# Plain slabs and weight sums of channel mixers 1 to 3 made one mixer ahead and kept in DRAM, in a two-layer decoder trunk on Trainium2

## The chip, the cores and the metric

The kernel runs on one core of a Trainium2 chip (trn2). The metric is the device time in microseconds of one execution, as the median of several runs. The core's engines work side by side, each on its own list of instructions in order: PE (TensorE) multiplies, DVE (VectorE) and ACT (ScalarE) work on tiles, POOL (GpSimd) does small things and starts some transfers, SP (SyncE) starts nearly all loads. A tile lies in SBUF, or in PSUM where PE writes it; DRAM is reached by DMA only.

## The reference

x has 512 tokens of 1024 numbers in fp32. Two layers follow, each with a channel mixer, a token mixer (latent attention in the first layer, sparse attention in the second) and another channel mixer, and a last norm ends it:

```
h = h + 1/2 * SwiGLU_a(RMSNorm(h))
h = h + Mixer_i(RMSNorm(h))
h = h + 1/2 * SwiGLU_b(RMSNorm(h))

def swiglu(x, w_gate, w_up, w_down):
    return (jax.nn.silu(x @ w_gate) * (x @ w_up)) @ w_down
```

The hidden width of SwiGLU is 2816. So there are four channel mixers, numbered 0 to 3 here; 0 opens layer 0, 1 closes it, 2 opens layer 1, 3 closes it.

## The kernel before

**Numbers.** Every fp32 operand of a matmul is split in two: ACT copies it to a rounded `hi` (L176, for a slab of weights L149), DVE subtracts that from the source for `lo` (L177, L151). Each product is then three matmuls: hi·hi, hi·lo, lo·hi (L168 to L170, L367 to L369, L379 to L381).

**A channel mixer** (`ffn`, L383) goes through the hidden width in 22 blocks of 128. The first blocks (`PLAIN`: 3 in mixer 0, 2 in the others) are *plain*: the gate slab (z = 0) and the up slab (z = 1) of a block, 128x1024 each, are loaded by SP (512 KB, tile wr, two buffers), split into one of three rotating weight tiles w0 to w2, and multiplied, 48 matmuls of 128x256 columns each.

The blocks behind them take seven products instead of eight (a Strassen-Winograd scheme of 2x2 blocks). `wsums` loads a block's gate slab rg and up slab ru, DVE makes four sums of halves (L353: s1; L354: into ru; L356, L357: into rg), and slabs and sums are split into the operands w[1] to w[7]. In the first product block ru, like every rg, lies in the ring `fr` with three buffers, in the others in wr; s1 has one buffer. `combine` makes the matching combinations of the input (tiles y, u and `four`; L242 to L244). The products run in the order 1, 7, 6, 2, 5, 4, 3, with 12 matmuls of 128x256 each; between them ACT copies px to pg (L497), pq to uq (L499) and px to uq (L501). Product 6 writes px again, so it waits for L497. uq has one buffer.

Product 1 needs only rg's split. Product 7 needs ru's, after a sum; product 6 that of the sums in rg.

**The norm.** The gate needs each token's 1/rms as a row. POOL takes a power (L282), DVE transposes the result (L290), two small POOL transfers spread it over the partitions (L291, L293). Then the plain blocks are finished (`plain_acts`, issued in the first product block): DVE multiplies the gate by the row (L395), ACT takes silu (L396), DVE multiplies by the row again (L397) and by the up half (L406, tile tu), ACT and DVE split that (ah, al).

**The down projection** runs in units of three blocks (wdr loads L425, matmuls, add L419), eight units spread over each three blocks.

**What sets the order.** The instructions of each engine are put in order by the scheduler of the tile framework, before the run; the program's text, priorities and `issue_after` lines steer it. On the chip each engine, and each queue of loads, keeps that order: an instruction that waits holds all that stand behind it. A load that waits for a buffer to come free also holds all behind it on SP.

Of the kernel before, what the change touches and what calls it, by code (L numbers as in the profile page):

```python
# [11 lines left out]
F32 = mybir.dt.float32  # L12
# [3 lines left out]
ALU = mybir.AluOpType  # L16
AX = mybir.AxisListType

P = 128
S = 512  # L20
D = 1024
KC = D // P
# [25 lines left out]
HS = S // 2  # L48
KP = KC // 2
PLAIN = 3, 2, 2, 2  # L50
PAD = 16
URGENT = 400
SHIFT = 1, 5, 7
TILES = 24
XC = P + 2
NG = 3
# [4 lines left out]
def f32v(ap):  # L61
    return ap.bitcast(F32)


class Kern:
# [13 lines left out]
    def setup(self):  # L79
        nc, cp, a = self.nc, self.cp, self.a  # L80

        self.nw, self.odd, self.nq = 0, 0, 0
        self.first = self.wp.tile([P, 2048 + 3 * PAD], F32R, tag="w0", name="w")
        small = self.wp.tile([P, 80], F32, name="small")
        self.vtc, self.small_sums, self.stc = small[:, :12], small[:, 12:16], small[:, 32:]
        self.sts, self.nst = [small[:, 12 + 4 * i : 16 + 4 * i] for i in range(5)], 0
        self.gains = cp.tile([P, 64], F32, name="gains")
        nc.scalar.dma_start(self.gains[:, :53], a["gains"])  # L90
        self.ident = cp.tile([P, P], F32, name="ident")
        nc.scalar.dma_start(self.ident, a["c_ident"])
        self.ones = cp.tile([P, P], F32R, name="ones")
        nc.vector.memset(f32v(self.ones), 1.0)
        nc.scalar.dma_start(self.gains[:, 53:57], a["c_rvalid"])
        tiny = self.gains[:, 57:62]
        nc.scalar.activation(tiny[:, 0:1], f32v(self.ones)[:, 0:1], AF.Copy)
        self.tiny = tiny
        self.root = self.gains[:, 62:63]
        nc.gpsimd.memset(self.root, -0.5)  # L100

        self.ngains = cp.tile([P, 32], F32, name="ngains")
        for i, x in enumerate(FGAINS):
            nc.vector.tensor_scalar(self.ngains[:, 8 * i : 8 * i + 8], self.gains[:, GAINS[x] : GAINS[x] + 8], -1.0, None, op0=ALU.mult)
        self.h, self.ahead, self.softmax, self.turn, self.chain, self.chained = [], [], False, 0, None, False
        self.h = [self.hp.tile([P, S], F32, name=f"h{c}") for c in range(KC)]
# [93 lines left out]
    def norm_split(self, c):  # L200
        t = self.xp.tile([P, 2 * S], F32R, tag="x", bufs=KC, name="x")
        if self.to_ffn:

            g = self.ngains[:, self.nng + c : self.nng + c + 1]
            v = t.rearrange("p (e z n) -> p e z n", e=2, z=2)
            hi, lo, src = v[:, :, 0, :], v[:, :, 1, :], self.h[c].rearrange("p (e n) -> p e n", e=2)
            self.split(src, hi, lo, gain=g)
            for e in range(2):
                self.xc["LR"[e], c] = v[:, e, 0, :], v[:, e, 1, :]
        else:  # L210
            self.split(self.h[c], t[:, :S], t[:, S:], gain=self.gains[:, self.ng + c : self.ng + c + 1])
            self.xh.append(t[:, :S])
            self.xl.append(t[:, S:])
# [104 lines left out]
    def sum_tiles(self, n):  # L318
        self.nsum += 1
        hi = self.fp.tile([P, n], F32R, tag="fh", bufs=3, name="wh")  # L320
        return hi, self.fp.tile([P, n + 2 * PAD], F32R, tag="fl", bufs=3, name="wl")[:, 2 * PAD :]

    def wsums(self, idx, f):


        nc, fp, w_gu = self.nc, self.fp, self.a["w_gu"]
        rg = fp.tile([P, 1024], F32, tag="fr", bufs=3, name="rg")
        nc.sync.dma_start(rg, w_gu[idx, f, 0])
        if f == PLAIN[idx]:

            ru = fp.tile([P, 1024], F32, tag="fr", bufs=3, name="ru")
        else:
            ru = self.wp.tile([P, 1024], F32, tag="wr", bufs=2, name="wr")
        nc.sync.dma_start(ru, w_gu[idx, f, 1])
        s1 = fp.tile([P, S], F32, tag="s1", bufs=1, name="s1")
        g0, g1, u0, u1 = rg[:, :S], rg[:, S:], ru[:, :S], ru[:, S:]

        def split(src, pool, tag, bufs):
            n = src.shape[1]
            if pool is self.wp:  # L340
                hi, lo = self.wtiles("half")
            elif n == 1024:
                hi, lo = self.sum_tiles(n)
            else:
                hi = pool.tile([P, n], F32R, tag=tag[0], bufs=bufs, name="wh")
                lo = pool.tile([P, n + 2 * PAD], F32R, tag=tag[1], bufs=bufs, name="wl")[:, 2 * PAD :]
            self.split(src, hi, lo)
            return [(hi[:, x : x + S].rearrange("p (k c) -> p k c", c=P), lo[:, x : x + S].rearrange("p (k c) -> p k c", c=P))
                    for x in range(0, n, S)]

        w = {}
        w[1], w[2] = split(rg, self.wp, None, 2)
        nc.vector.tensor_tensor(s1, u0, u1, op=ALU.add)  # L353
        nc.vector.tensor_tensor(u0, u0, g0, op=ALU.add)  # L354
        w[7], w[4] = split(ru, fp, ("fh", "fl"), 3)
        nc.vector.tensor_tensor(g0, g0, s1, op=ALU.add)  # L356
        nc.vector.tensor_tensor(g1, g1, g0, op=ALU.add)  # L357
        w[6], w[3] = split(rg, fp, ("fh", "fl"), 3)
        w[5], = split(s1, fp, ("sh", "sl"), 2)
        return w  # L360

    def product(self, j, w, out, first, last):
        mm = self.nc.tensor.matmul
        wh, wl = w[j]
        for p in range(KP):
# [2 lines left out]
            mm(out, wh[:, p], xl, start=False, stop=False, skip_group_check=True)  # L368
            mm(out, wl[:, p], xh, start=False, stop=last and p == KP - 1, skip_group_check=True)  # L369

    def plain(self, idx, f, z, out):

        wh, wl = self.ahead.pop(0) if self.ahead else self.wslab(self.a["w_gu"][idx, f, z], (KC, P), "half")
        mm = self.nc.tensor.matmul
        for k in self.order:
            for e in range(2):
                (xh, xl), o = self.xc["LR"[e], k], out[:, e * HS : e * HS + HS]

                mm(o, wh[:, k], xh, start=(k == 0 and e == 0), stop=False, skip_group_check=True)  # L379
                mm(o, wh[:, k], xl, start=False, stop=False, skip_group_check=True)  # L380
                mm(o, wl[:, k], xh, start=False, stop=(k == KC - 1), skip_group_check=True)  # L381

    def ffn(self, idx, gain_next, ap, tp):  # L383
        nc, a = self.nc, self.a
# [97 lines left out]
        for f in range(plain, NF):  # L482
# [3 lines left out]
            n = -(-len(units) // left)  # L486
# [23 lines left out]
            for work, tag in zip(todo, "oTS"):  # L510
                work(tag, copied if tag == "S" else None)
            act(f)
        if gain_next == "fin":

            hs, out = [self.parts(self.four(F32)) for _ in range(4)], []
            for t in range(4):
                for b in range(2):
                    p = self.mm_bank("ph")
                    for c in range(4):
                        nc.tensor.transpose(p[:, c * P : (c + 1) * P], self.h[4 * b + c][:, t * P : (t + 1) * P], self.ident)  # L520
                    out.append(hs[t][b])
                    nc.scalar.activation(out[-1], p, AF.Copy)
            return self.last(a["w_last"], ah, al, ap, out, hs)
# [921 lines left out]
```

## Time and profile before

| | us |
|---|---|
| median of 3 runs | 1857.13 (1856.23 to 1857.48) |
| the profiled execution | 1856.59 |
| its span, first to last instruction | 1854.8 |
| PE busy in it | 1834.9 |
| DVE busy | 1529.3 |
| ACT busy | 1091.9 |

A row of a group of instructions in the profile gives the line, the engine, the operation, out<-in, the shape, the count and the busy time. In a timeline the columns are the start and the length in us, and in brackets stands how long the engine was idle before it and for what. Tiles are named as in the program. Mean granted clock of the core: 0.999 of full speed.

### The profile page before, as it was taken

The numbers are of one execution on the slowest core, as the hardware profiler recorded it, in microseconds if no ns is written. First come the engines' busy times: TensorE is split into PE (matmuls) and PEld (weight loads), VectorE is DVE, ScalarE is ACT, GpSimd is POOL, SyncE is SP. The second block draws the span as 40 slices with busy tenths as digits, with TensorE's granted clock in tenths as the row PEclk, the third lists the DMA queues.
The fourth block names the chain that finished last, engine by engine and source line by source line (L and its number), as shares of the span: only waits on it lengthen the run. The fifth ranks groups of instructions, "written<-read, shape, count | busy, mean of one in ns | idle before, by whom it ended". The sixth has DMA issues, their size and how long they took to land.

```text
span 1854.8 us, 32725 instructions
## 1 busy us (share of the span) xinstructions
PE 1834.9 (99%) x12392; PEld 1675.0 (90%) x12392; DVE 1529.3 (82%) x2773; ACT 1091.9 (59%) x2030; POOL 251.5 (14%) x350
## 2 busy tenths in 40 slices
PE   8999999999999999999999999999999999999998
PEld 8999999888889999998999999988888889999997
DVE  7988886588789988887998888755988989988885
ACT  8555554489776555555655555426977865555554
POOL 0000000156510000000000000015665500000000
PEclk9999999999999999999999999999999999999999
DMA  7333333142333333333233333233222124333321
GB/s 259 118 103 102 103 107 108 56 107 71 96 115 113 104 110 111 111 106 100 97 116 107 107 104 97 90 106 108 75 86 75 46 106 137 103 107 103 103 91 57
DMA packets 79213, 191.12 MB, mean 103 GB/s; under 512 B 10024, under 2 KB 38080, under 8 KB 79056
## 3 DMA queue, kind: packets, MB, share of 16 engines
q1 hardware_dynamic: 75280, 182.42, 31.1%
q10 hardware_dynamic: 3104, 5.03, 0.8%
q8 instruction: 97, 1.59, 0.3%
q0 software_dynamic: 672, 1.59, 0.3%
q14 instruction: 60, 0.49, 0.1%
HBM read 179.75 MB, written 2.18 MB: 98 GB/s over the span
## 4 chain that ended last, share of the span: by engine, by line
PE 86%; DVE 8%; ACT 3%; issue 1%; DMA 1%; POOL 0%; SPq 0%; ACTq 0%; POOLq 0%; DVEq 0%
PE pd L168 8%; PE pd L170 8%; PE pd L169 8%; PE px L367 5%; PE px L369 5%; PE px L368 5%; PE pg L367 4%; PE pg L369 4%; PE pg L368 4%; PE pq L369 4%; PE pq L368 4%; PE pq L367 4%; PE o L1248 2%; PE pt L1223 2%; PE po L168 2%; PE po L170 2%
## 5 line engine op out<-in xcount | busy, mean ns | idle before, releaser
L169 PE MATMUL pd<-al,wd 128*128 128x512 f32 x576 | 224.1, 389 | 0.0
L168 PE MATMUL pd<-ah,wd 128*128 128x512 f32 x576 | 224.0, 389 | 0.0
L170 PE MATMUL pd<-ah,wd 128*128 128x512 f32 x576 | 224.0, 389 | 0.0
L177 DVE TENSOR_TENSOR w<-rg,w 128x1024 fp32r<-128x1024 f32 x79 | 96.6, 1223 | 104.4 <-ACT w L176 104.4
L367 PE MATMUL px<-four,wh 128*128 128x256 f32 x632 | 175.5, 278 | 4.0 <-ACT pg L497 3.8
L367 PE MATMUL pq<-four,wh 128*128 128x256 f32 x632 | 174.5, 276 | 0.3 <-DVE tu L406 0.3
L369 PE MATMUL px<-four,wl 128*128 128x256 f32 x632 | 174.7, 276 | 0.1
L368 PE MATMUL px<-four,wh 128*128 128x256 f32 x632 | 174.6, 276 | 0.0
L368 PE MATMUL pq<-four,wh 128*128 128x256 f32 x632 | 174.4, 276 | 0.0
L369 PE MATMUL pq<-four,wl 128*128 128x256 f32 x632 | 174.4, 276 | 0.0
L419 DVE SCALAR_TENSOR_TENSOR h<-pd,h 128x512 f32<-128x512 f32 x216 | 147.4, 683 | 6.0 <-PE pd L170 6.0
L176 ACT ACTIVATE wd<-wdr 128x384 fp32r<-128x384 f32 x192 | 98.5, 515 | 66.9 <-PE pd L169 35.9
L170 PEld LDWEIGHTS pd<-ah,wd 128*128 128x128 f32 x576 | 108.1, 188 | 22.5
L168 PEld LDWEIGHTS pd<-ah,wd 128*128 128x128 f32 x576 | 108.1, 188 | 19.5
L169 PEld LDWEIGHTS pd<-al,wd 128*128 128x128 f32 x576 | 108.1, 188 | 19.5
L367 PEld LDWEIGHTS px<-four,wh 128*128 128x128 f32 x632 | 118.6, 188 | 5.6 <-ACT pg L497 4.9
L367 PEld LDWEIGHTS pq<-four,wh 128*128 128x128 f32 x632 | 118.6, 188 | 0.5 <-ACT w L176 0.5
L369 PEld LDWEIGHTS px<-four,wl 128*128 128x128 f32 x632 | 118.6, 188 | 0.3 <-DVE wl L177 0.3
L369 PEld LDWEIGHTS pq<-four,wl 128*128 128x128 f32 x632 | 118.6, 188 | 0.0
L368 PEld LDWEIGHTS px<-four,wh 128*128 128x128 f32 x632 | 118.6, 188 | 0.0
L368 PEld LDWEIGHTS pq<-four,wh 128*128 128x128 f32 x632 | 118.6, 188 | 0.0
L176 ACT ACTIVATE w<-rg 128x1024 fp32r<-128x1024 f32 x79 | 83.7, 1060 | 57.5 <-PE pg L369 54.5
(363 smaller groups left out, 5942.1 us busy)
## 6 DMA issues: line engine op xcount, KB each, us to landing
wr<-in_w_gu SPq DMA_DIRECT2D x93, 512.0 KB, 4.1
rg<-in_w_gu SPq DMA_DIRECT2D x79, 512.0 KB, 3.3
wdr<-in_w_down SPq DMA_DIRECT2D x192, 192.0 KB, 2.4
wdr<-in_w_down SPq DMA_DIRECT2D x24, 256.0 KB, 2.7
wr<-in_mla_w_o SPq DMA_DIRECT2D x8, 512.0 KB, 3.5
wr<-in_nsa_w_q SPq DMA_DIRECT2D x8, 512.0 KB, 3.6
th<-btab_d SPq DMA_DIRECT2D x16, 256.0 KB, 3.6
wr<-in_nsa_w_o SPq DMA_DIRECT2D x8, 512.0 KB, 3.5
```

Of the source, the lines that this page charges most:

```text
L168: mm(out, wh, xh, start=first, stop=False)
L169: mm(out, wh, xl, start=False, stop=False)
L170: return mm(out, wl, xh, start=False, stop=last)
L176: nc.scalar.activation(hi, src, AF.Copy)
L177: (nc.gpsimd if pool else nc.vector).tensor_tensor(lo, src, f32v(hi), op=ALU.subtract)
L367: mm(out, wh[:, p], xh, start=first and p == 0, stop=False, skip_group_check=True)
L368: mm(out, wh[:, p], xl, start=False, stop=False, skip_group_check=True)
L369: mm(out, wl[:, p], xh, start=False, stop=last and p == KP - 1, skip_group_check=True)
L419: nc.vector.scalar_tensor_tensor(self.h[c], p, 0.5, self.h[c], op0=ALU.mult, op1=ALU.add)
L1223: nc.tensor.transpose(pt[:, j * P : j * P + P], p_sb[:, j * P : j * P + P], self.ident)
L1248: mm(out, vs[g][:, j, br * P : (br + 1) * P], x, start=False, stop=last and t == 1 and j == 2 * z + 1, skip_group_check=True)
```

## The change

It has two parts, both for mixers 1, 2 and 3, and both are worked in the product blocks of the mixer in front.

1. *Made slabs* (`make_load`, `make`, `made_slab`). In blocks 5 to 13 of mixers 0, 1 and 2 the next mixer's four plain slabs are loaded in halves (128x512, tile wm, eight in all), split by ACT and DVE into the right halves of the input tiles x of chunks 0 to 3 (`quarter`), and written, hi and lo, by two POOL transfers each to a DRAM tile `made`. In the next mixer one SP transfer of 1 MB brings hi and lo of a slab straight into a weight tile (L421), where before a load of 512 KB and a split by ACT and DVE stood.

2. *Presums* (`presum`). In blocks 4 to 11 of mixers 0, 1 and 2 the four half-sums of the next mixer's first two product blocks are made by transfers alone: POOL copies a half slab from DRAM to DRAM, waits for it, and adds a second one with an accumulating transfer (L335, L336). Each pair stands behind a small POOL copy that reads uq (L567, the *mark*). `wsums` then loads the sums: a half of ru, rs in two halves (from the ring fr) and s1, and DVE makes no sums for those two blocks.

The lines move: L176/L177 become L179/L180, L290 L294, L353 to L357 L382 to L386, L395 and L397 L448 and L450, L406 L459, L497/L499 L550/L552.

```diff
+READY = 5
+AHEAD = 2
+FIRST = 4
...
+            self.quarter[c] = t[:, S:]
...
+    def presum(self, idx, i):
+        g, w, z, f = self.nc.gpsimd, self.a["w_gu"], i % 4, PLAIN[idx] + i // 4
+        half = lambda x, e: w[idx, f, x][:, e * S : e * S + S]
+        pre = self.pre.setdefault((idx, f), [])
+        first, add = ((half(1, 0), half(1, 1)), (half(1, 0), half(0, 0)), (half(0, 0), pre and pre[0]), (half(0, 1), pre and pre[-1]))[z]
+        pre.append(self.dp.tile([P, S], F32, name=f"ws{z}{f}{idx}")[:, :])
+        g.dma_start(pre[z], first)
+        g.dma_start(pre[z], add, accum_op=ALU.add, max_dma_last_dim=4 * S)
...
-        nc.sync.dma_start(rg, w_gu[idx, f, 0])
+        self.gate_load = nc.sync.dma_start(rg, w_gu[idx, f, 0])
...
-        nc.sync.dma_start(ru, w_gu[idx, f, 1])
         s1 = fp.tile([P, S], F32, tag="s1", bufs=1, name="s1")
+        pre = self.pre.get((idx, f))
+        if pre:
+            nc.sync.dma_start(ru[:, :S], pre[1])
+            nc.sync.dma_start(ru[:, S:], w_gu[idx, f, 1][:, S:])
+            rs = fp.tile([P, 1024], F32, tag="fr", bufs=3, name="rs")
+            for e in range(2):
+                nc.sync.dma_start(rs[:, e * S : e * S + S], pre[2 + e])
+            nc.sync.dma_start(s1, pre[0])
+        else:
+            nc.sync.dma_start(ru, w_gu[idx, f, 1])
...
         w[1], w[2] = split(rg, self.wp, None, 2)
+        if pre:
+            w[7], w[4] = split(ru, fp, ("fh", "fl"), 3)
+            w[6], w[3] = split(rs, fp, ("fh", "fl"), 3)
+            w[5], = split(s1, fp, ("sh", "sl"), 2)
+            return w
...
+    def make_load(self, idx, i):
+        self.raw = self.sp.tile([P, S], F32, tag="s2", bufs=2, name="wm")
+        with self.tc.issue_after(self.gate_load.ins):
+            self.nc.sync.dma_start(self.raw, self.a["w_gu"][idx, i // 4, i // 2 % 2][:, i % 2 * S : i % 2 * S + S])
+
+    def make(self, idx, i):
+        hi, lo = [self.quarter[2 * (i % 2) + x] for x in range(2)]
+        self.split(self.raw, hi, lo)
+        d = self.made_tile(idx, i // 4, i // 2 % 2).rearrange("p (z e n) -> p z e n", z=2, e=2)
+        for z, t in enumerate((hi, lo)):
+            self.nc.gpsimd.dma_start(d[:, z, i % 2, :], f32v(t))
+
+    def made_slab(self, idx, f, z):
+        wh, wl = self.wtiles("half")
+        both = bass.AP(tensor=wh.tensor, offset=wh.offset, ap=[list(wh.ap[0]), [wl.offset - wh.offset, 2], [1, 1024]])
+        self.nc.sync.dma_start(f32v(both), self.made[idx, f, z].rearrange("p (z n) -> p z n", z=2))
...
-        wh, wl = self.ahead.pop(0) if self.ahead else self.wslab(self.a["w_gu"][idx, f, z], (KC, P), "half")
+        wh, wl = self.ahead.pop(0) if self.ahead else self.made_slab(idx, f, z) if idx else self.wslab(self.a["w_gu"][idx, f, z], (KC, P), "half")
...
+            if FIRST <= f < FIRST + 4 * AHEAD and idx + 1 < len(PLAIN):
+                mark = nc.gpsimd.tensor_copy(self.gains[:, 63:64], uq[:, HS : HS + 1])
+                with self.tc.issue_after(mark.ins):
+                    self.presum(idx + 1, f - FIRST)
+            if idx + 1 < len(PLAIN):
+                i = f - READY
+                if 0 < i <= 4 * PLAIN[idx + 1]:
+                    self.make(idx + 1, i - 1)
+                if 0 <= i < 4 * PLAIN[idx + 1]:
+                    self.make_load(idx + 1, i)
```

**DVE at the start of mixer 1**, from the finish of the plain blocks on. Before, tg is the gate of a plain block, rg_6555 and ru_6557 belong to the first product block, rg_6705 and wr_6707 to the second:

```order
L395 TENSOR_TENSOR tg_6579<-pg_6282,row_6280 128x512
L177 TENSOR_TENSOR wl_6566<-ru_6557,wh_6565 128x1024
L357 TENSOR_TENSOR rg_6555<-rg_6555 128x512
L395 TENSOR_TENSOR tg_6589<-pg_6283,row_6280 128x512
L397 TENSOR_TENSOR tg_6579<-tg_6579,row_6280 128x512
L177 TENSOR_TENSOR w_6710<-rg_6705,w_6710 128x1024
L177 TENSOR_TENSOR wl_6572<-rg_6555,wh_6571 128x1024
L406 SCALAR_TENSOR_TENSOR tu_6583<-pu_6284,tg_6579 128x512
L397 TENSOR_TENSOR tg_6589<-tg_6589,row_6280 128x512
L353 TENSOR_TENSOR s1_6709<-wr_6707 128x512
L177 TENSOR_TENSOR al_6586<-tu_6583,ah_6585 128x512
L406 SCALAR_TENSOR_TENSOR tu_6593<-pu_6428,tg_6589 128x512
```

In the change, with rs_6633 and s1_6630 of the first product block, rg_6778, wr_6780 and s1_6781 of the second:

```order
L180 TENSOR_TENSOR wl_6645<-rs_6633,wh_6644 128x1024
L180 TENSOR_TENSOR wl_6649<-s1_6630,wh_6648 128x512
L180 TENSOR_TENSOR four_6624<-u_6618,four_6624 128x1024
L448 TENSOR_TENSOR tg_6652<-pg_6366,row_6364 128x512
L448 TENSOR_TENSOR tg_6662<-pg_6367,row_6364 128x512
L180 TENSOR_TENSOR w_6788<-rg_6778,w_6788 128x1024
L180 TENSOR_TENSOR wl_6792<-wr_6780,wh_6791 128x1024
L450 TENSOR_TENSOR tg_6652<-tg_6652,row_6364 128x512
L450 TENSOR_TENSOR tg_6662<-tg_6662,row_6364 128x512
L459 SCALAR_TENSOR_TENSOR tu_6656<-pu_6368,tg_6652 128x512
L180 TENSOR_TENSOR wl_6800<-s1_6781,wh_6799 128x512
L459 SCALAR_TENSOR_TENSOR tu_6666<-pu_6506,tg_6662 128x512
```

The sums are gone, and the second block's ru and s1 splits have moved ahead of the second plain block's tu.

**ACT at the same place**, with the copy of product 1 (pg<-px, L497 and L550). Before:

```order
L396 ACTIVATE tg_6579<-tg_6579 128x512
L176 ACTIVATE wh_6571<-rg_6555 128x1024
L396 ACTIVATE tg_6589<-tg_6589 128x512
L454 ACTIVATE gains_77<-pg_6283,gains_77 128x1
L454 ACTIVATE gains_77<-pg_6282,gains_77 128x1
L176 ACTIVATE w_6889<-rg_6884 128x1024
L497 ACTIVATE pg_6603<-px_6601 128x256
```

In the change, with rg_6958 of the third product block:

```order
L449 ACTIVATE tg_6662<-tg_6662 128x512
L507 ACTIVATE gains_77<-pg_6367,gains_77 128x1
L179 ACTIVATE wh_6799<-s1_6781 128x512
L507 ACTIVATE gains_77<-pg_6366,gains_77 128x1
L179 ACTIVATE ah_6658<-tu_6656 128x512
L179 ACTIVATE w_6963<-rg_6958 128x1024
L179 ACTIVATE ah_6668<-tu_6666 128x512
L550 ACTIVATE pg_6676<-px_6674 128x256
```

The copy now stands behind both ah splits, whose source tu is DVE's.

**SP's loads at the start of mixer 1.** Before:

```order
L146 DMA wr_6482<-in_w_gu 128x1024
L328 DMA rg_6555<-in_w_gu 128x1024
L334 DMA ru_6557<-in_w_gu 128x1024
L328 DMA rg_6705<-in_w_gu 128x1024
L334 DMA wr_6707<-in_w_gu 128x1024
L334 DMA wr_6886<-in_w_gu 128x1024
L328 DMA rg_6884<-in_w_gu 128x1024
```

In the change, where `made` is a made slab and `ws` a presum:

```order
L343 DMA rg_6627<-in_w_gu 128x1024
L352 DMA ru_6629<-ws121_1084 128x512
L353 DMA ru_6629<-in_w_gu 128x512
L421 DMA w_6557<-made111_2373 128x2x1024
L356 DMA rs_6633<-ws221_1269 128x512
L356 DMA rs_6633<-ws321_1459 128x512
L357 DMA s1_6630<-ws021_918 128x512
L343 DMA rg_6778<-in_w_gu 128x1024
L356 DMA rs_6784<-ws231_2010 128x512
L356 DMA rs_6784<-ws331_2183 128x512
L343 DMA rg_6958<-in_w_gu 128x1024
L357 DMA s1_6781<-ws031_1631 128x512
```

The second block's s1 is the last of these loads, behind rs and the third block's rg.

More of the change, by code (lines that the diff above doesn't have):

```diff
@@ L80, in setup @@
         nc, cp, a = self.nc, self.cp, self.a
-        self.nw, self.odd, self.nq = 0, 0, 0
+        self.nw, self.odd, self.nq, self.made, self.quarter, self.pre = 0, 0, 0, {}, {}, {}
         self.first = self.wp.tile([P, 2048 + 3 * PAD], F32R, tag="w0", name="w")
@@ L369, in product, with made_tile @@
             mm(out, wl[:, p], xh, start=False, stop=last and p == KP - 1, skip_group_check=True)
+    def made_tile(self, idx, f, z):
+        if (idx, f, z) not in self.made:
+            self.made[idx, f, z] = self.dp.tile([P, 2048], F32, name=f"made{idx}{f}{z}")[:, :]
+        return self.made[idx, f, z]
+    def make_load(self, idx, i):
[12 more added lines that the diff above has]
+        self.nc.sync.dma_start(f32v(both), self.made[idx, f, z].rearrange("p (z n) -> p z n", z=2))
+        return [t.rearrange("p (k c) -> p k c", c=P) for t in (wh, wl)]
     def plain(self, idx, f, z, out):
-        wh, wl = self.ahead.pop(0) if self.ahead else self.wslab(self.a["w_gu"][idx, f, z], (KC, P), "half")
+        wh, wl = self.ahead.pop(0) if self.ahead else self.made_slab(idx, f, z) if idx else self.wslab(self.a["w_gu"][idx, f, z], (KC, P), "half")
         mm = self.nc.tensor.matmul
```

## The prediction, made before the change was timed

> **What bounds the kernel now.** I read the page's table of engines first, then the windows by stage, then the waits of PE, and last the timelines of the engines around each wait. The page's first part:
>
> ```profile
> PE 1834.9 (99%) x12392; PEld 1675.0 (90%) x12392; DVE 1529.3 (82%) x2773; ACT 1091.9 (59%) x2030; POOL 251.5 (14%) x350
> ```
>
> PE is busy for 1834.9 of 1854.8 us, so the matmuls set the time, and 20 us is all that any change that leaves them alone could bring. The windows say where those 20 us lie (columns: the window, its length, busy us of PE, PEld, DVE, ACT and POOL with counts, the granted clock, the DMA share, GB/s):
>
> ```profile
> 543.00:583.00 40.00, 38.22 (x334) 37.83 (x333) 38.23 (x58) 29.84 (x45) 3.09 (x3) 1.00 0.35 126
> 600.00:840.00 240.00, 240.00 (x1744) 225.50 (x1743) 204.13 (x313) 124.88 (x205) 0.00 (x0) 1.00 0.35 109
> ```
>
> In the middle of a channel mixer (600 to 840) PE never stops, and DVE, ACT and the DMAs have room: nothing taken off them there can help. At the start of mixer 1 (543 to 583) DVE is busy for 38.23 of 40 us and PE loses 1.8. The waits of PE name what it waits for (total us, times, longest):
>
> ```profile
> PE pg L379 <- ACT w L149: 5.7, 1, 5.7
> PE px L367 <- ACT pg L497: 3.8, 3, 1.7
> ```
>
> The 5.7 us are the program's first load, which the change leaves as it is. The 3.8 us are three waits, one in the first product block of each of mixers 1, 2 and 3: product 6 may not write px before ACT has copied product 1 out of it (L497). In PE's timeline (start, length) each shows as a hole between product 7's last matmul and product 6's first:
>
> ```profile
> 568.13 0.28 PE L368 MATMUL pq<-four,wh 128*128 128x256 f32 x1
> 568.24 0.28 PE L369 MATMUL pq<-four,wl 128*128 128x256 f32 x1
> 570.21 0.39 PE L367 MATMUL px<-four,wh 128*128 128x256 f32 x1 [1.69 <-ACT pg L497]
> ...
> 903.67 0.28 PE L369 MATMUL pq<-four,wl 128*128 128x256 f32 x1
> 904.71 0.39 PE L367 MATMUL px<-four,wh 128*128 128x256 f32 x1 [0.77 <-ACT pg L497]
> ...
> 1533.38 0.28 PE L369 MATMUL pq<-four,wl 128*128 128x256 f32 x1
> 1535.03 0.38 PE L367 MATMUL px<-four,wh 128*128 128x256 f32 x1 [1.37 <-ACT pg L497]
> ```
>
> One such matmul follows another after 0.11 us (568.13, 568.24), so the holes cost 1.86, 0.93 and 1.54 us. Four smaller ones stand in the blocks after; the first and the last:
>
> ```profile
> 580.00 0.28 PE L368 MATMUL px<-four,wh 128*128 128x256 f32 x1
> 580.36 0.38 PE L369 MATMUL px<-four,wl 128*128 128x256 f32 x1
> ...
> 936.30 0.28 PE L369 MATMUL pq<-four,wl 128*128 128x256 f32 x1
> 936.73 0.38 PE L367 MATMUL pg<-x,wh 128*128 128x256 f32 x1 [0.16 <-ACT pg L504]
> ```
>
> They cost 0.25 and 0.32; with the two between (0.21, 0.27) 1.05 us. So the change plays for 1.86 + 0.93 + 1.54 + 1.05 = 5.4 us, 0.3% of the time.
>
> Why is L497 late? ACT and DVE run in order, and L497 stands on ACT behind splits whose sources DVE has to deliver:
>
> ```profile
> 568.83 1.06 ACT L176 ACTIVATE w<-rg 128x1024 fp32r<-128x1024 f32 x1 [0.43 <-DMA rg<-in_w_gu]
> 569.79 0.37 ACT L497 ACTIVATE pg<-px 128x256 f32<-128x256 f32 x1
> ...
> 903.76 0.63 ACT L176 ACTIVATE ah<-tu 128x512 fp32r<-128x512 f32 x1 [0.61 <-DVE tu L406]
> 904.29 0.37 ACT L497 ACTIVATE pg<-px 128x256 f32<-128x256 f32 x1
> ```
>
> And DVE's whole chain hangs on the row of the norm: its transpose (L290) waits for POOL's power (L282), and DVE is idle for 0.93 to 0.95 us in front of it.
>
> ```profile
> 552.02 0.31 DVE L290 STREAM_TRANSPOSE row<-row 128x128 f32<-128x128 f32 x1 [0.93 <-POOL row L282]
> 552.26 0.38 DVE L244 TENSOR_TENSOR u<-y,u 128x256 f32<-128x256 f32 x1
> ...
> 558.51 1.22 DVE L177 TENSOR_TENSOR w<-rg,w 128x1024 fp32r<-128x1024 f32 x1
> 559.64 2.35 DVE L177 TENSOR_TENSOR four<-u,four 128x1024 fp32r<-128x1024 f32 x2
> ...
> 563.12 0.68 DVE L356 TENSOR_TENSOR rg<-rg,s 128x512 f32<-128x512 f32 x1
> 563.72 0.68 DVE L395 TENSOR_TENSOR tg<-pg,row 128x512 f32<-128x512 f32 x1
> ```
>
> ```profile
> 576.09 0.42 DVE L505 TENSOR_TENSOR tu<-px,uq 128x256 f32<-128x256 f32 x1
> 576.42 0.41 DVE L507 TENSOR_TENSOR tu<-pq,uq 128x256 f32<-128x256 f32 x1
> ```
>
> From start to start a 128x1024 operation holds DVE for 1.13 us (558.51, 559.64), a 128x512 one for 0.60, a 128x256 one for 0.33, the transpose for 0.24.
>
> **Start of mixers 1 and 3.** The change removes from DVE, ahead of the transpose, the plain blocks' splits and the first sums; but DVE stands idle there for POOL anyway, so what is taken off it before 552.02 brings nothing. What counts is what stands between the transpose and the second plain block's product (L406, in the change L459). In the change's order I count nine 128x1024 operations (four for the input's combinations, rg, ru and rs of the first block, rg and ru of the second), nine of 128x512, four of 128x256 and the transpose: 9 × 1.13 + 9 × 0.60 + 4 × 0.335 + 0.24 = 17.2 us. The second block's rg and ru are new in that stretch: the scheduler pulled them up into the room. So DVE ends at 552.02 + 17.2 = 569.2, where before the first product ended at 570.2 and L497 did not wait for DVE at all. In the change L550 (L497's new number) stands on ACT behind both ah splits: 0.53 (903.76 to 904.29) and 0.37, and PE goes on at about 570.2, against 570.21 before. In mixer 3 the transpose starts at 1516.77, and 17.2 + 0.9 gives 1534.9 against 1535.03.
>
> The power is the first unknown:
>
> ```profile
> 550.11 1.87 POOL L282 TENSOR_TENSOR row<-small,gains 128x4 f32<-128x4 f32 x1 [30.18 <-DVE small L279]
> ...
> 552.63 0.64 POOL L291 DMA_DIRECT2D nrow<-row  x1 [0.64 <-DVE row L290]
> ```
>
> ```profile
> 885.13 1.09 POOL L282 TENSOR_TENSOR row<-small,gains 128x4 f32<-128x4 f32 x1 [30.04 <-DVE small L279]
> ```
>
> The same operation took 1.87 us in mixer 1 and 1.09 in mixer 2. In the change only a 128x256 DVE operation stands beside it in mixers 1 and 3; if it then takes 1.09, both chains start 0.8 sooner. I take half of that in each: −0.4 in mixer 1 (ends −0.8 and 0.4), −0.5 in mixer 3 with its 0.1 (ends −0.9 and 0.4).
>
> [...]
>
> **Start of mixer 2.** There the order differs: the first block's rg split is DVE's sixth 128x1024 operation after the transpose.
>
> ```profile
> 886.25 0.31 DVE L290 STREAM_TRANSPOSE row<-row 128x128 f32<-128x128 f32 x1 [0.94 <-POOL row L282]
> ```
>
> It ends at 886.25 + 0.24 + 6 × 1.13 + 0.60 + 4 × 0.335 = 895.2, and only then does it free the buffer (fr has three) into which the second block's rg is loaded. What loads take:
>
> ```profile
> rg<-in_w_gu SPq DMA_DIRECT2D x79, 512.0 KB, 3.3
> ```
>
> ```profile
> DMA packets 519, 1.88 MB, mean 269 GB/s; under 512 B 63, under 2 KB 63, under 8 KB 518
> ...
> ru<-in_w_gu SPq DMA_DIRECT2D x1, 512.0 KB, 5.7
> ```
>
> (The first is the page's median over the program, the others are the DMAs from 542 to 549.) With 3.3 for the load and 0.96 for ACT's split (568.83 to 569.79) DVE can have it at 899.45, but is there four operations on (1.13 + 3 × 0.60 = 2.9), at 898.1: a new wait of 1.35. Seven operations on (2 × 1.13 + 5 × 0.60 = 5.3) and 0.9 of ACT, PE goes on at 905.7 against 904.71: +1.0. If the load is not waited for, −0.4; with 1 us more of it, +2.
>
> **The later holes and mixer 0.** By the next block DVE no longer makes four sums of 0.60 and is some 5 us ahead (it has the second block's rg and ru already), so I take the 1.05 as gone (ends −1.05 and 0). In mixer 0 the largest hole of the first product block is
>
> ```profile
> 42.44 0.28 PE L369 MATMUL px<-x,w 128*128 128x256 f32 x1
> 43.00 0.36 PE L367 MATMUL pq<-four,wh 128*128 128x256 f32 x1 [0.29 <-DVE tu L406]
> ```
>
> 0.45 us (0.56 − 0.11), behind DVE, whose order changes there too; and the first two splits of the making stand ahead of L550 on ACT, 0.53 each. I take +0.5, half of those, with ends 1.1 (both on the path) and −1.0 (the holes there close).
>
> **Costs that I put at nothing.** The making adds eight splits per mixer, 0.60 of DVE and 0.53 of ACT each, in the stretch in which DVE has 240 − 204.13 = 36 us free over sixteen blocks of 108 matmuls (1744 in 240 us, so 14.9 us a block): covered by 2.2 us a block. If that were not so, each would cost up to 0.6, 14 us in all. Eight blocks in each of mixers 0, 1 and 2 gain a mark copy on POOL, a copy and an accumulating transfer, and some two transfers of made halves. SP's queue gains small loads there and loses no time that PE sees. The DMA share of 0.35 must rise: the presums read and write some 1.3 MB a block, the made halves another 0.8, beside the 109 GB/s × 14.9 us = 1.6 MB now. That is about 0.8 at the worst; loads with a buffer or two in hand get slower, which I put at nothing in the middle of a mixer.
>
> [...]
>
> **The sum.** −0.4 + 1.0 − 0.5 − 1.05 + 0.5 = −0.45 us on the profiled execution's 1856.59, so 1856.1. The median of three is 1857.13, 0.54 above the profiled one: **1856.7**. All ends at once give −4.15 and +3.9 (1853.0 to 1861.0); the terms are independent, so I hold 1854 to 1860 for this case alone.
>
> **Rivals.** *Full relief.* The order says little of waits: if ACT, with fewer splits, has both ah halves early and the power is short, all seven holes close: 5.4 less, 1851.7. For it: the four sums really are gone from DVE's tightest 40 us. Against: the count of 17.2 above. 0.18.
>
> *Late loads (slower).* In mixers 1 and 3 the second block's rg goes out when the first's split is done, by the order 7.5 us after the transpose (559.5), and behind it on SP stand rs in two halves, the third block's rg and s1: 1.75 MB, and s1's split stands on DVE ahead of the second L459, so it must be there by 567.4. At 269 GB/s it takes 6.8 us and is in time; at 3.3 us per 512 KB, one after the other, 11.6. Beyond 7.9 us each microsecond counts twice. At 11.5 it costs 3.6 in each mixer: −0.45 + 7.2, 1863.9. For it: the made slabs of 1 MB double what is loaded in this stretch. Against: loads overlap, as the 269 GB/s show. 0.15.
>
> *POOL's chain (slower).* uq has one buffer, so ACT's L552 of the next block waits for POOL's mark copy, which stands in POOL's queue behind accumulating transfers that each wait for a copy to land, and behind the made halves. POOL per block: about 0.1 + 4 × 0.64 (the row at 552.63) and one landing, 1.65 as in the norm's row below or 5.7 as ru's, is 4.3 to 8.4 us against a period of 14.9.
>
> ```profile
> 554.92 0.58 POOL L293 DMA_DIRECT2D row<-nrow  x1 [1.65 <-DMA nrow<-row]
> ```
>
> It decides once that passes about 12 us; each microsecond beyond costs 24 (24 marks), so 13 us a block gives some 1881. Against it is the distance. 0.08.
>
> [...]
>
> **How the numbers follow.** The forecast has 0.59. A measurement of this kernel can tell about 0.2% (3.7 us) from no change; the forecast's own range lies within it nearly whole. Faster by more is full relief, 0.18; slower by more is late loads, POOL's chain and the forecast's upper tail, 0.25; the rest, 0.57, is the same. The range takes in full relief and late loads and leaves out POOL's chain and what lies past them: 1851.5 to 1864.
>
> **What would show it.** Right: the transposes at about 552.0 and 1516.8, L459 of the second block ending 17 us later, PE's holes ahead of product 6 in mixers 1 and 3 about as long as before, that of mixer 2 near 2 us with DVE waiting for rg ahead of it, and 240 of 240 busy in the middle. Wrong: a power of 1.1 us and no holes (full relief); DVE waiting for s1 or rg for over 2 us (late loads); ACT's L552 waiting for POOL in block after block (POOL's chain); or holes in the middle of mixers 0 to 2, which none of my terms has.

## The result, and the profile after

The changed kernel took 1871.67 us (median of 6 runs, 1866.39 to 1875.74), the kernel before 1857.17 in the same comparison: a ratio of 1.0074 with a 95% interval of 1.0056 to 1.0092. It is 14.5 us slower where no change was forecast, and outside the range. The profiled execution took 1872.23, with a span of 1870.5, 15.7 more than before.

The waits of PE in the changed kernel (total us, times, longest; L550 is what L497 was):

```profile
PE px L396 <- ACT pg L550: 10.6, 9, 2.7
PE pg L432 <- ACT w L152: 5.7, 1, 5.7
PE pg L396 <- ACT pg L557: 2.4, 2, 1.7
```

The same pair of lines as before, but nine waits instead of three, and 10.6 us instead of 3.8. The windows say where they are:

```profile
543.00:583.00 40.00, 39.21 (x316) 37.89 (x315) 36.39 (x55) 29.03 (x44) 3.42 (x5) 1.00 0.66 227
600.00:840.00 240.00, 236.89 (x1703) 222.19 (x1702) 201.22 (x309) 123.25 (x204) 20.25 (x36) 0.99 0.48 143
```

The start of mixer 1 is not where the time went (PE 39.21 of 40 busy, 38.22 before; the work there comes 5 to 6 us later now). The middle, in which PE had never stopped, has lost 3.1 us of PE time, and in 240 us it did 1703 matmuls instead of 1744. At 240 / 1744 = 0.138 us each the 41 missing ones are 5.6 us: some 2.5 us are lost while PE counts as busy.

The largest hole in that stretch, in PE's timeline:

```profile
676.79 0.28 PE L397 MATMUL pq<-four,wh 128*128 128x256 f32 x1
676.90 0.28 PE L398 MATMUL pq<-four,wl 128*128 128x256 f32 x1
679.23 0.38 PE L396 MATMUL px<-four,wh 128*128 128x256 f32 x1 [2.06 <-ACT pg L550]
679.45 0.33 PE L397 MATMUL px<-four,wh 128*128 128x256 f32 x1
679.58 0.42 PE L398 MATMUL px<-four,wl 128*128 128x256 f32 x1
679.79 0.41 PE L396 MATMUL px<-four,wh 128*128 128x256 f32 x1
680.00 0.41 PE L397 MATMUL px<-four,wh 128*128 128x256 f32 x1
```

and on ACT at that time:

```profile
675.21 0.63 ACT L179 ACTIVATE ah<-tu 128x512 fp32r<-128x512 f32 x1 [1.88 <-DVE tu L461]
678.28 0.63 ACT L179 ACTIVATE x<-wm 128x512 fp32r<-128x512 f32 x1 [2.44 <-DMA wm<-in_w_gu]
678.81 0.37 ACT L550 ACTIVATE pg<-px 128x256 f32<-128x256 f32 x1
```

ACT stands idle for 2.44 us for the load of wm, the quarter slab that is to be made, and the copy that PE needs stands directly behind its split. The waits of ACT say how often (total, times, longest):

```profile
ACT x L179 <- DMA wm<-in_w_gu: 32.5, 19, 3.1
```

The second thing to see is behind the hole: the matmuls follow at 0.21 us instead of 0.11. The granted clock in two windows there:

```profile
676.00:679.00 3.00, 1.18 (x11) 0.98 (x9) 1.51 (x4) 0.72 (x2) 0.00 (x0) 1.00 0.77 291
680.00:682.00 2.00, 2.00 (x11) 2.00 (x11) 0.92 (x2) 0.05 (x1) 0.53 (x1) 0.50 0.65 262
```

The clock falls to one half for some 3.4 us behind the hole; sixteen matmuls at 0.21 cost about 1.7 us more. The hole at 1017.21 (2.91 us) has the same tail. Taking PE's progress at equal counts of matmuls, mixer 0 lost 6.5 us, the middle of mixer 1 some 5.3, mixer 2 with its start 5.6, and the stretches with the starts of mixers 1 and 3 gained 0.9 and 0.8.

### The profile page after: what moved, and what is told of

Read it like the earlier page. It is cut to its first block, busy times and chain, and to the rows that moved or that the text cites. A ratio compares the mean times of both kernels' runs of the same rounds, so it can differ in the third digit from the quotient of the medians.

```text
span 1870.5 us, 33105 instructions
## 1 busy us (share of the span) xinstructions
PE 1840.7 (98%) x12392; PEld 1679.2 (90%) x12392; DVE 1517.8 (81%) x2761; ACT 1092.2 (58%) x2042; POOL 321.0 (17%) x470
## 5 line engine op out<-in xcount | busy, mean ns | idle before, releaser
L180 DVE TENSOR_TENSOR w<-rg,w 128x1024 fp32r<-128x1024 f32 x79 | 96.6, 1223 | 113.8 <-ACT w L179 113.8
L396 PE MATMUL px<-four,wh 128*128 128x256 f32 x632 | 176.8, 280 | 11.1 <-ACT pg L550 10.6
L397 PE MATMUL px<-four,wh 128*128 128x256 f32 x632 | 175.4, 278 | 0.0
L397 PE MATMUL pq<-four,wh 128*128 128x256 f32 x632 | 174.5, 276 | 0.0
L179 ACT ACTIVATE wd<-wdr 128x384 fp32r<-128x384 f32 x192 | 98.6, 515 | 70.8 <-PE pd L172 32.7
L396 PEld LDWEIGHTS px<-four,wh 128*128 128x128 f32 x632 | 119.4, 189 | 13.6 <-ACT pg L550 12.9
L179 ACT ACTIVATE w<-rg 128x1024 fp32r<-128x1024 f32 x79 | 83.7, 1060 | 62.3 <-PE pg L398 62.0
L397 PEld LDWEIGHTS px<-four,wh 128*128 128x128 f32 x632 | 119.4, 189 | 0.0
L397 PEld LDWEIGHTS pq<-four,wh 128*128 128x128 f32 x632 | 118.6, 188 | 0.0
```

The source lines that it names most:

```text
L179: nc.scalar.activation(hi, src, AF.Copy)
L180: (nc.gpsimd if pool else nc.vector).tensor_tensor(lo, src, f32v(hi), op=ALU.subtract)
L396: mm(out, wh[:, p], xh, start=first and p == 0, stop=False, skip_group_check=True)
```

## The experiments

The first theory (A) was the one that the lines above suggest: ACT's split of wm waits for its load and stands ahead of L550. The rival (B) was that the transfers on POOL's queue crowd the others. Three kernels took the change apart, a fourth was to test the clock by itself.

**Presums only.** Edit:

```diff
-        wh, wl = ... else self.made_slab(idx, f, z) if idx else self.wslab(...)
+        wh, wl = ... else self.wslab(...)
...
-                    self.make(idx + 1, i - 1)
-                    self.make_load(idx + 1, i)
```

> Only the presums stay; the plain slabs are loaded and split as before, nothing is made ahead. Theory A (the holes of PE in the middle of mixers 0 to 2 come from ACT's split of wm, which waits for its load and stands ahead of the copy L550): without that split no hole over 0.5 us in the middle of a mixer, the granted clock at full speed there, 1855 to 1859 us. Theory B (the transfers that POOL adds crowd the others out and hold POOL's queue): the presums are two thirds of POOL's added work and stay, so the holes stay too, in part: 1862 us or more.

Measured: 1854.62 us against 1857.65, ratio 0.9985 (0.9976 to 0.9994): faster than the kernel before; of the kernels here that load nothing in vain it is the only one. Its middle is without holes although POOL's presums are all there:

```profile
600.00:850.00 250.00, 250.00 (x1819) 234.93 (x1818) 206.74 (x317) 128.73 (x212) 12.34 (x22) 1.00 0.42 120
```

and at the starts the copy is waited for less than half as long as before:

```profile
PE px L396 <- ACT pg L550: 1.7, 3, 0.7
```

**Made slabs only.** Edit: `AHEAD = 0`, so no presums.

> Only the made slabs stay; no presums, so the weight sums are made by DVE as before and POOL has only the writes of the halves. Theory A: ACT's split of wm still stands ahead of L550 and the load of wm is still sent 12 us or less before it, so holes stay in the middle of mixers 0 to 2, shorter where the load lands sooner without POOL's transfers: 1859 to 1868 us. Theory B: with the presums the holes go: 1855 to 1859 us.

Measured: 1862.97, ratio 1.0033 (1.0020 to 1.0046). The making by itself loses 5.3 us; holes of 0.36 to 1.08 us stand in the middles. wm takes 3.9 us to land (median) instead of 4.9, and ACT waits for it for 12.4 us in all instead of 32.5. So the presums, which gain when they are alone, make the loss larger when they stand beside the making.

**The split moved behind the copy of product 5.** Edit:

```diff
+        with self.tc.issue_after(behind.ins):
             self.split(self.raw, hi, lo)
...
-                    self.make(idx + 1, i - 1)
+                    self.make(idx + 1, i - 1, copied)
```

> The whole change, with one more rule of order: ACT's split of wm stands behind the copy of product 5 (L557) of its block, so that L550 no longer stands behind it. All loads, splits and transfers are as many as in the change. Theory A: the holes in the middle of mixers 0 to 2 go (none over 0.5 us), 12 us of holes and some 4 us of halved clock come back: 1854 to 1858 us. Theory B: the same transfers crowd the same loads: 1864 us or more. A third case is that the load of wm, now waiting for its buffer on SP, holds the loads behind it: then holes stand where PE waits for ACT's or DVE's split of rg or wr.

Measured: 1867.93, ratio 1.0054 (1.0038 to 1.0071). A miss for theory A as I had put it: wm's split no longer stands ahead of the copy (L551 in this kernel), and the time did not come back. The waits of ACT show what took its place:

```profile
ACT wd L179 <- DMA wdr<-in_w_down: 59.2, 30, 4.2
```

The rule of order made the scheduler put a split of wd ahead of the copy instead, and that one waits for its load, wdr, up to 4.2 us.

**Graded holes.** Edit, in the kernel before, mixer 1 only:

```diff
+            for _ in range(DELAY.get(f, 0) if idx == 1 else 0):
+                nc.scalar.activation(uq[:, HS:], x, AF.Copy)
             nc.scalar.activation(g[:, :HS], x, AF.Copy)
```

> The kernel before, with 5 to 14 extra ACT copies of px ahead of L497 in every second product block of mixer 1 (blocks 6 to 20), so that PE has eight holes of graded length there and no transfer is added. About 0.31 us a copy: holes from about 0.5 to 3.5 us. Theory A on the clock (a hole of over about 2 us, and nothing else, halves the granted clock for some 3 us behind it): full clock behind the holes below 1.9 us, 0.5 behind those above 2.2 us, each of these costing about 1.7 us beyond its own length. The rival (the clock fell because of the higher load of the DMA or by chance): no halved clock here at all.

Measured: 1865.14 (one run), no hole in the middle over 0.5 us and no halved clock. The experiment failed: the scheduler saw the delay coming and put down-projection matmuls into it. Mixer 1 became some 8 us longer by many short pauses, and so the run tells nothing of the clock.

With theory A damaged I formed theory C: crowding, several transfers in the same few microseconds, makes all loads land late, and whichever split of a load stands ahead of L550 waits. Three kernels changed the amount of transfers.

**Half the rate.** Edit: a quarter and a half-sum in every second block, in blocks 5 to 20.

> The whole change at half the rate: a quarter is loaded, split and written in every second block (5 to 20), a half-sum is made in every second block (5 to 19), the written halves fall into the blocks between. Splits, loads and transfers are as many as in the change, and ACT's split of wm stands ahead of L550 as there. Theory C (crowding: loads, presums and writes that fall into the same few microseconds land 1 to 2 us later than they would alone, and the split that waits for such a load stands ahead of L550): shorter holes, none over 2 us in the middle of mixers 0 to 2, no halved clock: 1856 to 1863 us. Theory A (the place of wm's split is enough, whatever else moves): as many holes as in the change, 1866 us or more.

Measured: 1863.31, ratio 1.0026 (1.0017 to 1.0036), between the two expectations. A hole of 2.37 us stands in mixer 0, and ACT waits for wm for 33.9 us, as long as in the change. wm lands in 5.4 us (median), not sooner than the change's 4.9, though the transfers come at half the rate; that speaks against theory C.

**No writes of the made halves.** Edit: the two POOL transfers of `make` are left out, and plain slabs are loaded as before.

> The whole change without the writes of the made halves; the plain slabs are loaded and split as before, so the loads and splits of wm are work for nothing. Presums as in the change. Theory C: a fifth to a third of the added transfers is gone, landing of wm falls from 5.4 to about 4.5 us, holes shorter but there: 1858 to 1865 us. Theory A: wm's load and split stand where they stood, holes as in the change: 1866 us or more. If the writes alone had crowded the loads, no holes: 1854 to 1857 us.

Measured: 1866.28, ratio 1.0045 (1.0031 to 1.0060): at the lower end of theory A, above C. Without the writes 8.8 of the 14.5 us of loss are still there, so the loss does not need them.

**Copies for nothing.** Edit, in the kernel before:

```diff
+COPIES = 2, 4, 6
...
+            if 4 <= f < 20 and idx < 3:
+                mark = nc.gpsimd.tensor_copy(self.gains[:, 63:64], uq[:, HS : HS + 1])
+                with self.tc.issue_after(mark.ins):
+                    for k in range(COPIES[idx]):
+                        nc.gpsimd.dma_start(self.dp.tile([P, S], F32, name=f"sink{k}{f}{idx}")[:, :], self.a["w_gu"][idx, f, k % 2][:, :S])
```

> The kernel before, and POOL copies half slabs of 256 KB from DRAM to DRAM for nothing in blocks 4 to 19, behind a mark as in the change: 2 a block in mixer 0, 4 in mixer 1, 6 in mixer 2, none in mixer 3. No load, split or wait of ACT, DVE and SP is added. Theory C: the crowding by itself makes loads land late; wdr's split stands ahead of L497 in many blocks, so holes come with the dose: none or few in mixer 0, some in mixer 1, holes of 1 to 3 us in mixer 2: 1860 us or more in all. Theory A: without the split of wm nothing waits: 1855 to 1859 us.

Measured: 1857.54 against 1857.49, ratio 0.9999 (0.9989 to 1.0009). Its middles of mixers 1 and 2:

```profile
600.00:850.00 250.00, 250.00 (x1819) 234.95 (x1818) 209.02 (x321) 128.75 (x212) 36.36 (x79) 1.00 0.55 174
950.00:1180.00 230.00, 230.00 (x1670) 216.01 (x1669) 194.23 (x297) 118.85 (x195) 50.26 (x104) 1.00 0.66 209
```

At 209 GB/s, where the change moves 143, PE does not stop once. (PE in 600 to 850 does 1819 matmuls here, with the presums alone, and in the kernel before.) So transfers by themselves, on POOL's queue too, cost PE nothing, and theories B and C fall as causes by themselves. The run shows less than I had expected of it, though: a split of wd stands directly ahead of L497 not in many blocks but in one (the table below). Whether transfers lengthen the waits of a split that does stand there, it does not test; the made slabs alone, where wm lands 1 us sooner and the loss is smaller, suggest that they do.

Theory D then said that it is the place of wm's load among SP's loads, together with that of a waiting split ahead of the copy. Three more kernels:

**The load moved behind the block's last wdr, the split behind the copy of product 5.** Edit:

```diff
-        with self.tc.issue_after(self.gate_load.ins):
+        with self.tc.issue_after(self.wdr_load.ins):
...
+        with self.tc.issue_after(behind.ins):
             self.split(self.raw, hi, lo)
```

> The whole change, with two rules of order: the load of wm stands on SP behind the block's last load of wdr (and so in front of rg's wait for its buffer, with nothing urgent behind it), and its split stands on ACT behind the copy of product 5 (L557) of the next block, some 10 us later. All work and all transfers are as in the change. Theory D (the loss comes from where the load of wm stands among SP's loads and where a split that waits for a load stands ahead of L550, not from the amount of work or of transfers): no hole over 0.5 us in the middle of mixers 0 to 2: 1852 to 1856 us, no slower than the presums alone (1854.6). Rival (the amount of added splits and transfers is too much for these blocks wherever they stand): 1860 us or more.

Measured: 1864.12, ratio 1.0047 (1.0032 to 1.0061): a miss. ACT again waits for wdr directly ahead of the copy:

```profile
655.31 0.61 ACT L179 ACTIVATE ah<-tu 128x512 fp32r<-128x512 f32 x1
659.98 0.52 ACT L179 ACTIVATE wd<-wdr 128x384 fp32r<-128x384 f32 x1 [4.05 <-DMA wdr<-in_w_down]
660.41 0.37 ACT L551 ACTIVATE pg<-px 128x256 f32<-128x256 f32 x1
```

**The load without the split.** Edit: as without the writes, and `self.split(self.raw, hi, lo)` left out; wm is loaded and not used.

> Presums as in the change, and wm is loaded as in the change, but nothing splits or writes it, and the plain slabs are loaded and split as before. Theory D: the load alone delays its neighbours on SP by about 1 us, wdr's among them, whose split stands ahead of L550 in some blocks: a few short holes, 1855 to 1858 us. Rival (the load of wm crowds out SP's other loads, and that is what PE waits for): holes as without the writes, 1862 us or more.

Measured: 1854.92, ratio 0.9987 (0.9978 to 0.9996), as with the presums alone. The load by itself, where the change has it on SP, costs nothing.

**The split without the load.** Edit: as without the writes, and `make_load` only for i = 0; all eight splits read that quarter.

> Presums as in the change, and ACT and DVE do the eight splits of wm per mixer, but of one quarter that is loaded once per mixer and stays; no writes, and the plain slabs are loaded and split as before. Theory D: a split that waits for no load costs nothing, as DVE and ACT have room: no holes over 0.5 us in the middle, 1854 to 1856 us. Rival (the added splits by themselves delay ACT's copies and DVE's sums): 1860 us or more.

Measured: 1859.16, ratio 1.0010 (1.0000 to 1.0019), 4.5 us above the presums alone. Neither side had that: a split that waits for no load still costs, by holes of 0.3 to 0.6 us. Ready at once, the splits were put into the first blocks, and eight of them directly ahead of a copy of px, here product 5's (L554 in this kernel, L557 in the change). Three of the eight are not free of waits either: ACT stands idle 0.6 to 0.8 us ahead of them, in the row below for DVE's half of another split:

```profile
96.36 0.63 ACT L179 ACTIVATE x<-wm 128x512 fp32r<-128x512 f32 x1 [0.82 <-DVE x L180]
96.89 0.37 ACT L554 ACTIVATE pg<-px 128x256 f32<-128x256 f32 x1
```

These rows led to the last theory (E): what costs is what stands directly ahead of a copy of px on ACT, because PE has only the 12 matmuls of one product (1.3 us) before it needs that copy: product 7's behind product 1, product 4's behind product 5. So I counted, in ACT's order of every kernel, the splits of wm or wd that stand directly ahead of a copy of px to pg:

| kernel | of wm | of wd | median us | ratio |
|---|---|---|---|---|
| before | 0 | 1 | 1857 to 1858 | 1 |
| copies for nothing | 0 | 1 | 1857.54 | 0.9999 |
| presums only | 0 | 2 | 1854.62 | 0.9985 |
| load without split | 0 | 2 | 1854.92 | 0.9987 |
| split without load | 8 | 2 | 1859.16 | 1.0010 |
| made slabs only | 12 | 2 | 1862.97 | 1.0033 |
| half the rate | 19 | 0 | 1863.31 | 1.0026 |
| load behind wdr | 0 | 10 | 1864.12 | 1.0047 |
| no writes | 16 | 0 | 1866.28 | 1.0045 |
| split behind product 5 | 0 | 10 | 1867.93 | 1.0054 |
| the change | 14 | 0 | 1871.67 | 1.0074 |

In the change thirteen of the fourteen stand ahead of product 1's copy and one ahead of product 5's. All kernels in the table that stay behind the kernel before have eight or more of wm or of wd, the others two or fewer in all. The count doesn't give the size: half the rate has 19 and loses less than the change with 14. That the size hangs on how late each load lands is likely but not shown. The test moves only the place:

**The split behind the second copy to uq.** Edit:

```diff
-            nc.scalar.activation(uq[:, HS:], x, AF.Copy)
+            self.third[f - plain] = nc.scalar.activation(uq[:, HS:], x, AF.Copy)
...
-        self.split(self.raw, hi, lo)
+        with self.tc.issue_after(self.third[i].ins):
+            self.split(self.raw, hi, lo)
```

> The whole change, with one rule of order: ACT's split of wm stands behind the second copy to uq (L554) of a product block instead of ahead of its first copy to pg (L550); the block is the same, and after L554 ACT waits about 1 us for PE in the kernel as changed. All work, loads and transfers are as in the change; no split of a loaded tile is moved ahead of L550 in its place (two wdr splits stand there, as with the presums alone). Theory E (what costs the time is that on ACT a split that waits for a load, or just takes 0.5 us, stands directly ahead of the copy of px for which PE waits; amount of work, of transfers and SP's order do not matter by themselves): no hole over 0.5 us in the middle of mixers 0 to 2, 1853 to 1856 us, within 2 us of the presums alone (1854.6). Rival (load, split and write together are too much, wherever the split stands): 1860 us or more.

Measured: 1857.69 against 1857.99, ratio 1.0001 (0.9992 to 1.0010). Of the change's 14.5 us all but what can't be measured came back, with every load, split and transfer still there. ACT waits for wm for 1.4 us in all instead of 32.5. It waits for wdr longer than in the change, 34.1 us instead of 18.5, and PE does not stop for that in the middles of mixers 1 and 2: what counts is the place of the wait. The middle of mixer 1, and ACT in one of its blocks:

```profile
600.00:850.00 250.00, 250.00 (x1819) 234.96 (x1818) 208.03 (x319) 129.27 (x215) 19.73 (x35) 1.00 0.48 144
```

```profile
673.02 0.39 ACT L555 ACTIVATE uq<-px 128x256 f32<-128x256 f32 x1 [0.92 <-PE px L398]
673.30 0.62 ACT L179 ACTIVATE x<-wm 128x512 fp32r<-128x512 f32 x1
674.38 1.06 ACT L179 ACTIVATE w<-rg 128x1024 fp32r<-128x1024 f32 x1 [0.46 <-PE pg L398]
```

The split lies in a gap in which ACT waits for PE anyway. The size was missed by 2 us: 1853 to 1856 was expected, and it stays 3 us behind the presums alone. Those 3 us stand mainly at the first product blocks (holes of 1.17 in mixer 0, 1.38 and 1.80 at the starts of mixers 1 and 3, where the presums alone have none over 0.5, 0.88 and 0.73) and in two further holes, of 0.86 in mixer 0 and 0.75 in mixer 2; why the starts are later was not tried.

**The same without presums.** Edit: `AHEAD = 0` in that kernel.

> The made slabs alone with the same rule of order, and no presums. Theory E: of the 5.8 us that the made slabs alone lost, those in the middle of mixers 0 to 2 come back; five splits of loaded tiles still stand ahead of copies of px, against 14: 1855 to 1858 us. Rival: 1860 us or more. Beside the run with the whole change it also tells what the presums bring when nothing disturbs them: about 2 us by the holes at the starts of mixers 1 to 3.

Measured: 1858.29, ratio 1.0002 (0.9993 to 1.0011), against 1862.97 without the rule of order: 4.7 us back, 0.3 short of what was expected. Five splits of loads (two of wm, three of wd) still stand directly ahead of copies of px there, and holes of 1.74 and 0.70 us in mixer 2 remain. Beside it the presums of the kernel above bring 0.6 us, which can't be told from nothing, where about 2 was expected.

## Why the prediction was wrong

**The step that failed** is "Costs that I put at nothing: the making adds eight splits per mixer ... covered by 2.2 us a block". The cover was counted as DVE's free time, and DVE does have it: it is busy for 201 of 240 us in the middle after the change. But the splits also stand on ACT, whose order is fixed, and there it is not the share that counts but what is next behind. Fourteen of them stand directly ahead of a copy of px. With wm landing 4.9 us after its issue (median) ACT waited for it nineteen times, 32.5 us in all, and the copies that PE needs waited behind it. With the same work and transfers, but the splits a few places later in ACT's order (split behind the second copy to uq), the time was 1857.69. The upper bound that I gave, 14 us if each split were paid in full, is the size of the loss by luck; its mechanism was another, for the most part a wait and not the work. The same paragraph holds the second mistake: the making's loads were held to be harmless because other loads have buffers in hand. The load is harmless (load without split), but not the instruction that waits for it where it stands. The DMA share, which I gave as about 0.8 at the worst, was 0.48 in the middle of mixer 1: only about half of its blocks carry the added transfers, and I counted the bytes of these both as read and as written, those of the loads before only once.

I had the means to see it. ACT's order of the changed kernel shows it in block after block, as here in mixer 1:

```
L179 ACTIVATE x_6200<-wm_7686 128x512
L550 ACTIVATE pg_6984<-px_6982 128x256
```

I used that only for the first product block of mixer 0, and there with half a microsecond. The last of my signs of being wrong, holes in the middle of mixers 0 to 2, is the one that came.

**The clock** is in none of my terms. Two holes over 2 us in the profiled execution cost about 1.7 us each beyond their length, and the six runs spread from 1866.39 (mean granted clock 0.999) to 1875.74 (0.996).

**Mixers 1 and 3** came out as worked out, up to the power. The chain from the transpose to the end of the second product (start, length):

```profile
557.27 0.31 DVE L294 STREAM_TRANSPOSE row<-row 128x128 f32<-128x128 f32 x1 [0.93 <-POOL row L286]
...
573.84 0.68 DVE L459 SCALAR_TENSOR_TENSOR tu<-pu,tg 128x512 f32<-128x512 f32 x1
```

573.84 + 0.60 − 557.27 = 17.2 us, the sum of the prediction. The power took the short end:

```profile
556.16 1.07 POOL L286 TENSOR_TENSOR row<-small,gains 128x4 f32<-128x4 f32 x1 [29.78 <-DVE small L283]
```

1.07 us where it was 1.87 with a 128x1024 DVE operation beside it (in mixer 3 1.09, and 1.89 before); now the operation beside it is a 128x256 one, as in mixer 2 before the change, where the power took 1.09. So the holes are 0.95 and 1.20 us (1.86 and 1.54 before): −0.9 and −0.3 where I took −0.4 and −0.5. The power is 0.80 us shorter in both mixers, of which I had taken half.

**Mixer 2**: the forecast of +1.0 took the wrong buffer. rg's split of the first block ends 9.0 us after the transpose, as worked out, but the load of the second block's rg does not wait for it. The timelines of DVE and SP, and SP's waits in 890 to 915, show for what it does:

```profile
897.10 0.31 DVE L294 STREAM_TRANSPOSE row<-row 128x128 f32<-128x128 f32 x1 [0.95 <-POOL row L286]
900.85 1.22 DVE L180 TENSOR_TENSOR wl<-ru,wh 128x1024 fp32r<-128x1024 f32 x1
902.09 0.33 SPq L343 DMA_DIRECT2D rg<-in_w_gu  x1
904.93 1.21 DVE L180 TENSOR_TENSOR w<-rg,w 128x1024 fp32r<-128x1024 f32 x1
909.00 1.21 DVE L180 TENSOR_TENSOR w<-rg,w 128x1024 fp32r<-128x1024 f32 x1
```

```profile
SPq L343 <- DVE wl L180: 6.0, 1, 6.0
```

The load goes out at 902.09, when DVE has split the first block's ru (900.85 + 1.13 = 901.98), and so 4 us ahead of the end of rg's split at 906.06; only the third block's rg is sent behind that. The load took 4.9 us, longer than the 3.3 of the prediction, and DVE still takes the second block's rg at 909.00 without a wait. The hole there is 0.99 against 0.93 before.

**The rivals.** Late loads lay nearest to the measured time with 1863.9, still 8 us short, and what happened was not its reason: s1 made ACT wait 1.2 to 2.0 us in mixers 1 and 2, but DVE's chain in mixer 1 ended on time. POOL's chain did not happen: no wait of ACT's L552 for POOL stands among the waits, and presums alone are a gain. Full relief, with holes smaller but not gone, is in part what the presums gave without the making: 3.0 us of its 5.4, and 2.3 with the load of wm beside them.

## What to carry to other kernels

A new instruction is not free because its engine has room: look in the engine's own order for what stands directly behind it, and ask how long the bottleneck can go on without that. An instruction that waits for a transfer belongs where its engine waits for the bottleneck anyway. And a rule of order must be checked in the new order as a whole, for the scheduler fills the place that it frees: twice here with another wait of the same kind.

## What the runs showed of the hardware

**PE's clock after a hole.** From the start of the last matmul ahead of a hole to the next matmul, spaces of 2.33 and 3.02 us (the change) and of 2.13 and 3.38 (split behind product 5) were each followed by a granted clock of 0.50. In the change it lasted 3.413 us each time by the clock records of the trace, with sixteen matmuls at 0.21 us, some 1.7 us lost. Spaces up to 1.97 us (the kernel before) were not followed by it. But with half the rate a space of 2.49 us was not either:

```profile
91.35 0.28 PE L398 MATMUL pq<-four,wl 128*128 128x256 f32 x1
93.83 0.39 PE L396 MATMUL px<-four,wh 128*128 128x256 f32 x1 [2.21 <-ACT pg L550]
94.06 0.28 PE L397 MATMUL px<-four,wh 128*128 128x256 f32 x1
94.18 0.28 PE L398 MATMUL px<-four,wl 128*128 128x256 f32 x1
```

There the granted clock was 1.00 from 91.3 to 94 and from 94 to 96. So the length of a hole alone does not decide; what else does, no run here shows.

**Transfers beside compute.** 209 GB/s for 230 us (copies for nothing, middle of mixer 2) did not stop PE once. They were not without effect: in that stretch wdr landed in 2.6 us instead of the 2.4 of the kernel before and rg in 4.5 instead of 3.3 (medians), and ACT waited for wdr for 29.9 us in the whole execution instead of 12.9, which in that stretch cost PE nothing (230.00 of 230 us busy).
